# Seven products for eight in half of an MLP's first matrix

## The chip, the cores and the metric

The kernel runs on one core of a Trainium2 chip. The metric is the device time of one execution in microseconds (us). The engines of the core are TensorE (PE in the profile, with its weight loads as PEld), VectorE (DVE), ScalarE (ACT), GpSimd (POOL) and SyncE (SP), each with an instruction queue of its own; SP, ACT and POOL issue DMAs.

## The reference

A trunk of two residual layers over 256 tokens of width 2048, batch 1, in float32. Layer 0 mixes tokens with differential attention, layer 1 with a Mamba-2 mixer; each is followed by an MLP of width 8192. What bears on the change is the MLP:

```python
def sq_relu_mlp(h, w1, w2):
    return jnp.square(jax.nn.relu(h @ w1)) @ w2

for i in range(DEPTH):                       # DEPTH = 2
    hn = rms_norm(h, mixer_norm[i])
    mix = diff_attention(hn, ...) if i % 2 == 0 else mamba2_mixer(hn, ...)
    h = h + mix
    h = h + sq_relu_mlp(rms_norm(h, mlp_norm[i]), mlp_w1[i], mlp_w2[i])
```

`w1` is 2048 x 8192, `w2` is 8192 x 2048.

## The kernel before, in words

All weights come from HBM once, in units of 128 partitions x 1024 float32 (512 KB). `load` (L169) issues the DMA of a unit on SP into a `raw` tile, of which there are six. `split_weights` (L147) makes two float32r parts of it: ScalarE writes the rounded part `wh` (L152), VectorE the remainder `wl = raw - wh` (L153); four buffers each. Activations are split in the same way into a rounded part and a remainder, side by side in an `act` tile. A product is then three matmul terms: rounded by rounded, and the two mixed ones.

There are two forms of a product:

- `sub_block` (L156), for projections whose result has features on partitions: the weights are the stationary side, the activations (both parts side by side, 512 columns) the moving one. Eight matmuls over 512 columns with `wh`, then eight over 256 columns with `wl`. `wide_pair` (L180) runs it four times for two output blocks of 128 features, `wide_one` (L189) twice for one. `add_sums` (L196) then adds the two halves of the bank.
- `token_block` (L202), for projections whose result has tokens on partitions: the activations are stationary, 512 columns of weights move. Per unit and block of 128 tokens: two rounded, two remainder and two mixed matmuls, 12 in all for 256 tokens.

`mlp` (L475) goes through the hidden width in four quarters of 2048. In a quarter the *up stage* makes eight pairs of hidden blocks with `wide_pair`, applies the squared ReLU (L485), and splits the result (`split_pair`, L227) into `hid`. The *down stage* runs `token_block` four times, once for every 512 output columns, over the eight units of `w2` that belong to the quarter, and adds into the residual `h` (L490), with the scale of the norm.

Small work (norm inputs, attention, the scan) is written as generators in a `Side` queue and is emitted by `side.tick()` between matmuls. `norm_input` (L250) transposes a part of `h` on PE and makes `xs`, the split inputs of the next projection, from it (`x_parts`, L235). The code is written against a tile framework: it gives out buffers and semaphores, and when the program is built it also orders each engine's instructions by its own model of time, with the order in the program as priority. On the chip every queue runs in that fixed order.

PSUM is held by two pools for the whole kernel: four banks for `pp`, three for `aux` and one for `aux1`.

Of the kernel before, what the change touches and what calls it, by code (L numbers as in the profile page):

```python
# [82 lines left out]
def wait(n):  # L83
    for _ in range(n):
        yield


@with_exitstack
def trunk_kernel(ctx: ExitStack, tc: tile.TileContext, x, xt, par, rope, qk, wv, wo, w10, w20, win, wdt, wout, w11, w21, out):
# [20 lines left out]
    G.affine_select(out=tri, in_=ones, pattern=[[1, P]], compare_op=ALU.is_ge, fill=0.0, base=0, channel_multiplier=-1)  # L110

    def aux():
        return ps_ax.tile([P, 512], F32, tag="aux", bufs=3, name="aux")

    def aux1():
        return ps_ax.tile([P, 512], F32, tag="aux1", bufs=1, name="aux1")

    def rows(dst, cols, name):

# [23 lines left out]
    def cols(j):  # L143
        return slice(NB * j, NB * (j + 1))


    def split_weights(raw, n=1):  # L147
        wh = wp.tile([P, 1024], F32R, tag="wh", bufs=4, name="wh")
        wl = wp.tile([P, 1024], F32R, tag="wl", bufs=4, name="wl")
        for i in range(n):  # L150
            s = slice(1024 // n * i, 1024 // n * (i + 1))
            S.copy(out=wh[:, s], in_=raw[:, s])  # L152
            V.tensor_tensor(out=wl[:, s], in0=raw[:, s], in1=wh[:, s].bitcast(F32), op=ALU.subtract)  # L153
        return wh, wl
# [13 lines left out]

    def load(src, n=1):  # L169

        raw = wp.tile([P, 1024], F32, tag="raw", bufs=6, name="raw")
        w = 1024 // n
        for i in range(n):
            nc.sync.dma_start(out=raw[:, i * w:(i + 1) * w], in_=src[:, i * w:(i + 1) * w])
        return raw

    def bank():
        return ps.tile([P, 2, T], F32, tag="mm", name="pp")
# [17 lines left out]
    def add_sums(dst, pp):  # L196

        for t in range(len(pp)):
            S.copy(out=dst[:, t, :], in_=pp[t][:, 1, :])  # L199
            V.tensor_tensor(out=dst[:, t, :], in0=pp[t][:, 0, :], in1=dst[:, t, :], op=ALU.add)  # L200

    def token_block(src, j, acts):  # L202

        pp = [bank().rearrange("p a b -> p (a b)") for _ in range(2)]
        n = src.shape[0]
        for s in range(n):
            w = split_weights(load(src[s, j]))
            for i, wi in enumerate(w):
                for k in range(2):
                    while len(acts) <= 2 * s + k:  # L210
                        side.tick()
                    act = acts[2 * s + k]
                    m = wi[:, k * NB:(k + 1) * NB]
                    for t in range(2):
                        tok = slice(t * P, (t + 1) * P)
                        PE.matmul(pp[t], lhsT=act[:, 0, tok], rhs=m, start=(s + i + k == 0), stop=(s == n - 1 and i + k == 2))  # L216
                        if i == 0:
                            PE.matmul(pp[t], lhsT=act[:, 1, tok], rhs=m, start=False, stop=False)  # L218
                    if i == 0 or k:
                        side.tick()  # L220
        return pp

    def act_pair():
        t = actp.tile([P, 2, 2, T], F32R, tag="act", bufs=16, name="act")
# [2 lines left out]
    def split_pair(src):  # L227

        t, parts = act_pair()
        S.copy(out=t[:, :, 0, :], in_=src)  # L230
        V.tensor_tensor(out=t[:, :, 1, :], in0=src, in1=t[:, :, 0, :].bitcast(F32), op=ALU.subtract)  # L231
        return parts
# [44 lines left out]
    def norm_mean():  # L277

        V.tensor_reduce(out=ms, in_=ssq, axis=AX.X, op=ALU.add)
        V.tensor_scalar(out=ms, in0=ms, scalar1=1.0 / D, scalar2=EPS, op0=ALU.mult, op1=ALU.add)  # L280

    def residual(pp, j):
        for t in range(2):
            V.tensor_tensor(out=h[:, t, cols(j)], in0=pp[t], in1=h[:, t, cols(j)], op=ALU.add)  # L284

    xs = []
    first = [bank() for _ in range(2)]
    raw = []  # L290
# [21 lines left out]
    with tc.tile_pool(name="att", bufs=1) as ap:  # L312
# [139 lines left out]
        for hd in range(NH):  # L452
            qkn = ap.tile([P, 4, T], F32, tag="qkn", bufs=2, name="qkn")
            pq = qkn[:, 0:2, :]
            add_sums(pq, wide_pair(qk, 4 * hd, xs) if hd else first)
            side.add(qk_norm(pq, qg, pq))
            pk = qkn[:, 2:4, :]
            add_sums(pk, wide_pair(qk, 4 * hd + 2, xs))
            st = []
            side.add(qk_work(pk, qkn, st))  # L460
            if hd % 2 == 0:
                v2 = ap.tile([P, 2, 2, T], F32, tag="v", bufs=2, name="v")
                for t, pv in enumerate(token_block(wv, hd // 2, xs)):
                    S.activation(v2[:, t], pv.rearrange("p (a b) -> p a b", a=2), AF.Identity, scale=rtok[:, t:t + 1])
            side.add(av_work(hd, v2[:, :, hd % 2, :], qkn, st, heads), slow=True)
        for j in range(4):
            residual(token_block(wo[0:4], j, sum((heads[i] for i in range(4)), [])), j)
        side.drain()
        xs = []
        for j in range(4):  # L470
            residual(token_block(wo[4:8], j, sum((heads[i] for i in range(4, 8)), [])), j)
            side.add(norm_input(j, C_MLP0, xs))


    def mlp(xs, w1, w2, pool, after):  # L475
        r2 = const.tile([P, 2], F32, tag="r2", bufs=2, name="r2")
        for q in range(4):
            hid = []
            for j in range(8):
                r = pool.tile([P, 2, T], F32, tag="relu", bufs=2, name="relu")  # L480
                add_sums(r, wide_pair(w1, 16 * q + 2 * j, xs))
                if q == 0 and j == 1:
                    norm_mean()
                    V.reciprocal(out=r2, in_=ms)
                V.scalar_tensor_tensor(out=r, in0=r, scalar=0.0, in1=r, op0=ALU.max, op1=ALU.mult)  # L485
                hid += split_pair(r)
# [12 lines left out]
            side.add(norm_input(j, C_MIX1, xs_next))  # L499

    with tc.tile_pool(name="mlp0", bufs=1) as mp:
        mlp(xs, w10, w20, mp, to_mixer)
    xs = xs_next


    with tc.tile_pool(name="ssm", bufs=1) as sp:
        dram_a = tc.dram_tile([64, T], F32, name="dram_a")
        rstd = sp.tile([P, T], F32, name="rstd")
# [220 lines left out]
        def out_part(q, last):  # L729
            acts = ys[2 * q] + ys[2 * q + 1]  # L730
            for j in range(4):
                residual(token_block(wout[4 * q:4 * q + 4], j, acts), j)
                if last:
                    side.add(norm_input(j, C_MLP1, xs_next))

# [10 lines left out]
        out_part(3, True)  # L746
    xs = xs_next

    with tc.tile_pool(name="mlp1", bufs=1) as mp:
        mlp(xs, w11, w21, mp, lambda j, t: nc.sync.dma_start(out=out[:, t, cols(j)], in_=h[:, t, cols(j)]))  # L750

def _units(b):

    return np.ascontiguousarray(b.reshape(b.shape[0], P, -1, 1024).transpose(0, 2, 1, 3))


def _blocks(w, order=None):

    k, n = w.shape[0] // P, w.shape[1] // P
    b = w.reshape(k, P, n, P).transpose(2, 1, 0, 3)
    if order is not None:
        b = b[order]
    return _units(b)


def _tokens(w):
# [69 lines left out]
```

## Time and profile before

| | us |
|---|---|
| Median of 3 runs (2512.38 to 2512.57) | 2512.4 |
| The profiled execution | 2510.96 |
| Span of it, first to last instruction | 2509.2 |
| PE busy | 2493.1 (99%) |
| DVE busy | 1668.7 (67%) |
| ACT busy | 1310.0 (52%) |
| POOL busy | 1.2 |
| Moved by DMA | 471.26 MB, mean 188 GB/s |

A group row of the profile reads: line, engine, operation, output <- inputs, shape, xcount | busy us, mean ns of one | idle time of the engine before them, and what ended it. In a timeline row the first number is the start in us, the second how long it took. In the chain of waits a row is a piece of the chain that ended last: its start and the time it gave to the chain. In a table of windows each engine has its busy time and, in brackets, its instructions; the last columns are the granted PE clock, the busy share of the 16 DMA engines, and GB/s.

### The profile page before, as it was taken

The numbers are of one execution on the slowest core, as the hardware profiler recorded it, in microseconds if no ns is written. First come the engines' busy times: TensorE is split into PE (matmuls) and PEld (weight loads), VectorE is DVE, ScalarE is ACT, GpSimd is POOL, SyncE is SP. The second block draws the span as 40 slices with busy tenths as digits, with TensorE's granted clock in tenths as the row PEclk, the third lists the DMA queues.
The fourth block names the chain that finished last, engine by engine and source line by source line (L and its number), as shares of the span: only waits on it lengthen the run. The fifth ranks groups of instructions, "written<-read, shape, count | busy, mean of one in ns | idle before, by whom it ended". The sixth has DMA issues, their size and how long they took to land.

```text
span 2509.2 us, 33804 instructions
## 1 busy us (share of the span) xinstructions
PE 2493.1 (99%) x13038; PEld 2122.0 (85%) x13038; DVE 1668.7 (67%) x2158; ACT 1310.0 (52%) x1919; POOL 1.2 (0%) x8
## 2 busy tenths in 40 slices
PE   8999999999999999999999999999999999999999
PEld 6888888888888888888888888888888888888887
DVE  7888876655555556558886887887665565555554
ACT  6656655434434434456776575674544443443443
POOL 0000000000000000000000000000000000000000
PEclk9999999999999999999999999999999999999999
DMA  8445555555555565556655556455555555656564
GB/s 276 163 157 181 167 176 183 187 193 193 187 193 191 187 199 187 190 179 207 196 186 195 175 188 207 159 186 187 184 190 193 192 186 193 193 188 193 189 197 139
DMA packets 131122, 471.26 MB, mean 188 GB/s; under 512 B 14640, under 2 KB 14832, under 8 KB 130960
## 3 DMA queue, kind: packets, MB, share of 16 engines
q1 hardware_dynamic: 127152, 458.28, 56.1%
q10 hardware_dynamic: 3808, 10.81, 1.3%
q8 instruction: 102, 1.67, 0.3%
q14 instruction: 60, 0.49, 0.1%
HBM read 466.88 MB, written 2.16 MB: 187 GB/s over the span
## 4 chain that ended last, share of the span: by engine, by line
PE 99%; DMA 1%; SPq 0%; issue 0%; DVE 0%; ACT 0%; DVEq 0%
PE pp L162 35%; PE pp L216 28%; PE pp L166 18%; PE pp L218 14%; PE aux L650 1%; PE aux L135 0%; PE aux L397 0%; PE aux L259 0%; DMA raw<-in_qk 0%; PE aux L620 0%; PE aux L651 0%; PE aux L426 0%; DMA xf<-in_x 0%; PE aux L427 0%; PE aux L607 0%; PE aux L420 0%
## 5 line engine op out<-in xcount | busy, mean ns | idle before, releaser
L153 DVE TENSOR_TENSOR wl<-raw,wh 128x1024 fp32r<-128x1024 f32 (+1 forms) x867 | 1057.2, 1222 | 711.0 <-ACT wh L152 704.8
L152 ACT CAST wh<-raw 128x1024 fp32r<-128x1024 f32 (+1 forms) x867 | 908.1, 1049 | 1074.1 <-PE pp L218 507.0
L162 PE MATMUL pp<-act,wh 128*128 128x512 f32 x3856 | 979.3, 394 | 11.8 <-DVE act L241 11.8
L162 PEld LDWEIGHTS pp<-act,wh 128*128 128x128 f32 x3856 | 693.0, 189 | 138.1 <-ACT wh L152 11.1
L216 PE MATMUL pp<-wh,act 128*128 128x512 f32 x1536 | 601.3, 391 | 0.0
L218 PE MATMUL pp<-wh,act 128*128 128x512 f32 x1536 | 599.0, 390 | 0.0
L166 PEld LDWEIGHTS pp<-act,wl 128*128 128x128 f32 x3856 | 524.6, 191 | 37.7 <-issue 1.7
L166 PE MATMUL pp<-act,wl 128*128 128x256 f32 x3856 | 540.8, 283 | 0.0
L216 PE MATMUL pp<-wl,act 128*128 128x512 f32 x1536 | 413.4, 391 | 0.0
L216 PEld LDWEIGHTS pp<-wh,act 128*128 128x128 f32 x1536 | 288.5, 188 | 60.2 <-issue 1.0
L218 PEld LDWEIGHTS pp<-wh,act 128*128 128x128 f32 x1536 | 288.8, 188 | 58.1
L216 PEld LDWEIGHTS pp<-wl,act 128*128 128x128 f32 x1536 | 286.6, 188 | 59.9 <-issue 1.0
L575 DVE SCALAR_TENSOR_TENSOR cy<-u,cwb,cy 128x256 f32<-128x256 f32 x144 | 62.5, 480 | 21.3 <-ACT cy L573 21.2
L490 DVE SCALAR_TENSOR_TENSOR h<-pp,r,h 128x512 f32<-128x512 f32 x64 | 45.1, 747 | 43.0 <-PE pp L216 43.0
L200 DVE TENSOR_TENSOR relu<-pp,relu 128x256 f32<-128x256 f32 x128 | 53.5, 418 | 0.0
L199 ACT COPY relu<-pp 128x256 f32<-128x256 f32 x128 | 46.9, 367 | 0.0
L485 DVE SCALAR_TENSOR_TENSOR relu<-relu 128x512 f32<-128x512 f32 x64 | 44.3, 692 | 2.2
L635 ACT ACTIVATE m<-ab,acol 128x128 f32<-128x128 f32 x128 | 41.6, 391 | 6.7 <-PE aux L651 6.7
L284 DVE TENSOR_TENSOR h<-pp,h 128x512 f32<-128x512 f32 x48 | 31.0, 685 | 19.7 <-PE pp L216 19.7
L231 DVE TENSOR_TENSOR act<-relu,act 128x512 fp32r<-128x512 f32 x64 | 43.9, 686 | 0.0
L230 ACT CAST act<-relu 128x512 fp32r<-128x512 f32 x64 | 39.2, 613 | 0.0
L240 ACT ACTIVATE act<-aux,pa 128x256 fp32r<-128x256 f32 x48 | 21.6, 472 | 12.4 <-DVE act L241 9.4
(175 smaller groups left out, 954.0 us busy)
## 6 DMA issues: line engine op xcount, KB each, us to landing
raw<-in_w SPq DMA_DIRECT2D x512, 512.0 KB, 4.0
raw<-in_win SPq DMA_DIRECT2D x160, 512.0 KB, 3.5
raw<-in_wout SPq DMA_DIRECT2D x64, 512.0 KB, 3.5
raw<-in_qk SPq DMA_DIRECT2D x63, 512.0 KB, 4.2
raw<-in_wv SPq DMA_DIRECT2D x32, 512.0 KB, 3.3
raw<-in_wo SPq DMA_DIRECT2D x32, 512.0 KB, 3.5
ab<-dram_a ACTq DMA_DIRECT2D x16, 512.0 KB, 5.1
xf<-in_x SPq DMA_DIRECT2D x8, 256.0 KB, 6.6
```

What stands on the lines that cost most here:

```text
L152: S.copy(out=wh[:, s], in_=raw[:, s])
L153: V.tensor_tensor(out=wl[:, s], in0=raw[:, s], in1=wh[:, s].bitcast(F32), op=ALU.subtract)
L162: PE.matmul(acc, lhsT=wh[:, k * P:(k + 1) * P], rhs=acts[k0 + k], start=(start and k == 0), stop=False)
L166: PE.matmul(acc[:, 0, :], lhsT=wl[:, k * P:(k + 1) * P], rhs=acts[k0 + k][:, 0, :], start=False, stop=(stop and k == 7))
L199: S.copy(out=dst[:, t, :], in_=pp[t][:, 1, :])
L200: V.tensor_tensor(out=dst[:, t, :], in0=pp[t][:, 0, :], in1=dst[:, t, :], op=ALU.add)
L216: PE.matmul(pp[t], lhsT=act[:, 0, tok], rhs=m, start=(s + i + k == 0), stop=(s == n - 1 and i + k == 2))
L218: PE.matmul(pp[t], lhsT=act[:, 1, tok], rhs=m, start=False, stop=False)
L231: V.tensor_tensor(out=t[:, :, 1, :], in0=src, in1=t[:, :, 0, :].bitcast(F32), op=ALU.subtract)
L485: V.scalar_tensor_tensor(out=r, in0=r, scalar=0.0, in1=r, op0=ALU.max, op1=ALU.mult)
L490: V.scalar_tensor_tensor(out=h[:, t, cols(j)], in0=pp[t], scalar=r2[:, t:t + 1], in1=h[:, t, cols(j)], op0=ALU.mult, op1=ALU.add)
L575: V.scalar_tensor_tensor(out=y[:, i, :], in0=u[:, i, k:k + T], scalar=cwb[:, w + k:w + k + 1], in1=y[:, i, :], op0=ALU.mult, op1=ALU.add)
```

## The change

Half of the hidden columns of a quarter (1024 of 2048, in both MLPs) are made by Strassen's method in its form with few additions (Winograd's): a 2 x 2 block product in seven block products. The blocks are 128 tokens x 128 inputs on the activations' side and 128 inputs x 512 columns on the weights' side; the seven results gather in seven PSUM banks over the eight pairs of input blocks (`seven`), and `seven_out` joins them to 256 tokens x 1024 columns. `sum_parts` makes the four sums on the activations' side once per MLP, as side work. On the weights' side four sums are needed: for two of them the block is first loaded twice by a broadcast DMA, and a DMA issued by GpSimd adds two other blocks to it; VectorE makes the other two. The result has tokens on partitions; `hidden` squares it, transposes it on PE in the down stage, and splits it.

The other half stays with `wide_one`. The two alternate; in the first quarter the seven products start two steps later. In the down stage the units that belong to the second half come first. The host prepares the mixed weight layout (`_mixed`). In the MLPs one PSUM pool with eight banks takes the place of the two pools. Loads have four `raw` buffers in place of six; `wh` and `wl` become one tile `w`, four buffers as before. The unread output `junk` of the norm's squares is bfloat16.

```diff
@@ trunk_kernel
-    ps = ctx.enter_context(tc.tile_pool(name="ps_mm", bufs=4, space=PSUM))
-    ps_ax = ctx.enter_context(tc.tile_pool(name="ps_ax", bufs=3, space=PSUM))
+    psum = {}
+    def psum_pools(stack, one):
+        psum["mm"] = stack.enter_context(tc.tile_pool(name="ps_mm", bufs=8 if one else 4, space=PSUM))
+        psum["ax"] = None if one else stack.enter_context(tc.tile_pool(name="ps_ax", bufs=3, space=PSUM))
...
     def split_weights(raw, n=1):
-        wh = wp.tile([P, 1024], F32R, tag="wh", bufs=4, name="wh")
-        wl = wp.tile([P, 1024], F32R, tag="wl", bufs=4, name="wl")
+        w = wp.tile([P, 2, 1024], F32R, tag="w", bufs=4, name="w")
+        wh, wl = w[:, 0, :], w[:, 1, :]
...
-        raw = wp.tile([P, 1024], F32, tag="raw", bufs=6, name="raw")
+        raw = wp.tile([P, 1024], F32, tag="raw", bufs=4, name="raw")
...
-            junk = const.tile([P, NB], F32, tag="junk", bufs=1, name="junk")
+            junk = const.tile([P, NB], BF16, tag="junk", bufs=1, name="junk")
...
+    def sum_parts(pool, x, dst):
+        a = pool.tile([P, 2, T], F32, tag="relu", bufs=2, name="a")
+        for i in range(2):
+            V.tensor_tensor(out=a[:, i, :], in0=x[i][:, 0, :].bitcast(F32), in1=x[i][:, 1, :].bitcast(F32), op=ALU.add)
+        a11, a21, a12, a22 = (a[:, i, t * P:(t + 1) * P] for i in range(2) for t in range(2))
+        f = pool.tile([P, 4, P], F32, tag="relu", bufs=2, name="asum")
+        yield
+        V.tensor_tensor(out=f[:, 0, :], in0=a21, in1=a22, op=ALU.subtract)
+        V.tensor_tensor(out=f[:, 1, :], in0=f[:, 0, :], in1=a11, op=ALU.subtract)
+        V.tensor_tensor(out=f[:, 2, :], in0=a11, in1=a21, op=ALU.subtract)
+        V.tensor_tensor(out=f[:, 3, :], in0=a12, in1=f[:, 1, :], op=ALU.add)
+        yield
+        sa = pool.tile([P, 2, 4, P], F32R, tag="sa", bufs=8, name="sa")
+        S.copy(out=sa[:, 0], in_=f)
+        V.tensor_tensor(out=sa[:, 1], in0=f, in1=sa[:, 0].bitcast(F32), op=ALU.subtract)
...
+    def seven(pool, src, acts, pp, start, stop):
+        r = pool.tile([P, 7, NB], F32, tag="raw7", bufs=2, name="raw7")
+        nc.sync.dma_start(out=r[:, 3:5, :], in_=src[:, 3:4, :].broadcast_to([P, 2, NB]))
+        nc.sync.dma_start(out=r[:, 0:3, :], in_=src[:, 0:3, :])
+        G.dma_start(out=r[:, 3:5, :], in_=src[:, 0:2, :], accum_op=ALU.add)
+        ws = []
+        def parts(a, n):
+            if n == 2:
+                w = wp.tile([P, 2, 2, NB], F32R, tag="w", bufs=4, name="w")
+            else:
+                w = pool.tile([P, 2, 1, NB], F32R, tag="w1", bufs=2, name="w1")
+            S.copy(out=w[:, 0], in_=r[:, a:a + n, :])
+            V.tensor_tensor(out=w[:, 1], in0=r[:, a:a + n, :], in1=w[:, 0].bitcast(F32), op=ALU.subtract)
+            for i in range(n):
+                ws.append((w[:, 0, i, :], w[:, 1, i, :]))
+        parts(0, 2)
+        parts(2, 2)
+        V.tensor_tensor(out=r[:, 5, :], in0=r[:, 1, :], in1=r[:, 3, :], op=ALU.add)
+        V.tensor_tensor(out=r[:, 6, :], in0=r[:, 5, :], in1=r[:, 2, :], op=ALU.add)
+        parts(4, 2)
+        parts(6, 1)
+        for n, ((ah, al), (wh, wl)) in enumerate(zip(acts, ws)):
+            PE.matmul(pp[n], lhsT=ah, rhs=wh, start=start, stop=False)
+            PE.matmul(pp[n], lhsT=al, rhs=wh, start=False, stop=False)
+            PE.matmul(pp[n], lhsT=ah, rhs=wl, start=False, stop=stop)
+            if n in (1, 3, 5, 6):
+                side.tick()
+
+    def seven_out(pool, pp):
+        p1, p3, p2, p5, p7, p6, p4 = pp
+        u = pool.tile([P, 2, 2, NB], F32, tag="raw7", bufs=2, name="u")
+        a = pool.tile([P, NB], F32, tag="relu", bufs=2, name="ua")
+        b = pool.tile([P, NB], F32, tag="relu", bufs=2, name="ub")
+        S.copy(out=a, in_=p1)
+        V.tensor_tensor(out=u[:, 0, 0], in0=p2, in1=a, op=ALU.add)
+        V.tensor_tensor(out=a, in0=p6, in1=a, op=ALU.add)
+        V.tensor_tensor(out=b, in0=p7, in1=a, op=ALU.add)
+        V.tensor_tensor(out=u[:, 0, 1], in0=p5, in1=a, op=ALU.subtract)
+        V.tensor_tensor(out=u[:, 0, 1], in0=p3, in1=u[:, 0, 1], op=ALU.add)
+        V.tensor_tensor(out=u[:, 1, 1], in0=p5, in1=b, op=ALU.subtract)
+        V.tensor_tensor(out=u[:, 1, 0], in0=p4, in1=b, op=ALU.add)
+        return u
...
+        def hidden(u, hid):
+            V.scalar_tensor_tensor(out=u, in0=u, scalar=0.0, in1=u, op0=ALU.max, op1=ALU.mult)
+            yield from wait(2)
+            uf = u.rearrange("p t a b -> p t (a b)")
+            for j in range(4):
+                ax = aux().rearrange("p (a b) -> p a b", a=2)
+                for f in range(2):
+                    for t in range(2):
+                        PE.transpose(ax[:, f, t * P:(t + 1) * P], uf[:, t, T * j + P * f:T * j + P * f + P], ident)
+                hid += split_pair(ax)
+                yield
+
+        side.add(sums_of(), slow=True)
         for q in range(4):
             hid = []
-            for j in range(8):
-                r = pool.tile([P, 2, T], F32, tag="relu", bufs=2, name="relu")
-                add_sums(r, wide_pair(w1, 16 * q + 2 * j, xs))
...
+            wait_for = 2 if q == 0 else 0
+            for j in range(8 + wait_for):
+                if j >= wait_for:
+                    i = j - wait_for
+                    while len(sas) <= i:
+                        side.tick()
+                    if i == 0:
+                        p7 = [bank().rearrange("p a b -> p (a b)") for _ in range(7)]
+                    seven(pool, w1s[q, i], sas[i], p7, i == 0, i == 7)
+                    if i == 7:
+                        u = seven_out(pool, p7)
+                if j < 8:
+                    if j % 2 == 0:
+                        r = pool.tile([P, 2, T], F32, tag="relu2", bufs=1, name="relu")
+                    add_sums(r[:, j % 2:j % 2 + 1], [wide_one(w1, 8 * q + j, xs)])
+                    if j % 2:
...
+                        V.scalar_tensor_tensor(out=r, in0=r, scalar=0.0, in1=r, op0=ALU.max, op1=ALU.mult)
+                        hid += split_pair(r)
+            side.add(hidden(u, hid))
             for j in range(4):
-                pp = token_block(w2[8 * q:8 * q + 8], j, hid)
+                src = rng(w2, 8 * q + 4, 8 * q + 8) + rng(w2, 8 * q, 8 * q + 4)
+                pp = token_block(src, j, hid)
```

More of the change, by code (lines that the diff above doesn't have):

```diff
@@ L112, in aux @@
     def aux():
-        return ps_ax.tile([P, 512], F32, tag="aux", bufs=3, name="aux")
+        if psum["ax"] is None:
+            return psum["mm"].tile([P, 512], F32, tag="mm", name="aux")
+        return psum["ax"].tile([P, 512], F32, tag="aux", bufs=3, name="aux")
     def aux1():
-        return ps_ax.tile([P, 512], F32, tag="aux1", bufs=1, name="aux1")
+        return psum["ax"].tile([P, 512], F32, tag="aux1", bufs=1, name="aux1")
     def rows(dst, cols, name):
@@ L177, in bank @@
     def bank():
-        return ps.tile([P, 2, T], F32, tag="mm", name="pp")
+        return psum["mm"].tile([P, 2, T], F32, tag="mm", name="pp")
     def wide_pair(src, b, acts):
@@ L204, in token_block @@
         pp = [bank().rearrange("p a b -> p (a b)") for _ in range(2)]
-        n = src.shape[0]
+        n = len(src)
         for s in range(n):
-            w = split_weights(load(src[s, j]))
+            w = split_weights(load(src[s][j]))
             for i, wi in enumerate(w):
@@ L221, in token_block, with rng @@
         return pp
+    def rng(src, a, b):
+        return [src[i] for i in range(a, b)]
     def act_pair():
@@ L466, in trunk_kernel @@
         for j in range(4):
-            residual(token_block(wo[0:4], j, sum((heads[i] for i in range(4)), [])), j)
+            residual(token_block(rng(wo, 0, 4), j, sum((heads[i] for i in range(4)), [])), j)
         side.drain()
@@ L470, in trunk_kernel @@
         for j in range(4):
-            residual(token_block(wo[4:8], j, sum((heads[i] for i in range(4, 8)), [])), j)
+            residual(token_block(rng(wo, 4, 8), j, sum((heads[i] for i in range(4, 8)), [])), j)
             side.add(norm_input(j, C_MLP0, xs))
-    def mlp(xs, w1, w2, pool, after):
-        r2 = const.tile([P, 2], F32, tag="r2", bufs=2, name="r2")
+    scope.close()
+    def sum_parts(pool, x, dst):
[13 more added lines that the diff above has]
+        V.tensor_tensor(out=sa[:, 1], in0=f, in1=sa[:, 0].bitcast(F32), op=ALU.subtract)
+        x0, x1 = x
+        s1, s2, s3, s4 = ([sa[:, i, n, :] for i in range(2)] for n in range(4))
+        dst.append([[x0[:, i, 0:P] for i in range(2)], s4, [x1[:, i, 0:P] for i in range(2)], s1, s3, s2, [x1[:, i, P:T] for i in range(2)]])
+        yield
@@ new lines, in mlp, with sums_of @@
+    def mlp(xs, w1, w1s, w2, pool, after):
+        r2 = const.tile([P, 2], F32, tag="r2", bufs=2, name="r2")
+        sas = []
+        def sums_of():
+            for j in range(KT // 2):
+                while len(xs) < 2 * j + 2:
+                    yield
+                yield from sum_parts(pool, xs[2 * j:2 * j + 2], sas)
+        def hidden(u, hid):
[8 more added lines that the diff above has]
+                hid += split_pair(ax)
+                yield
+        side.add(sums_of(), slow=True)
@@ L477, in mlp @@
         for q in range(4):
             hid = []
-            for j in range(8):
-                r = pool.tile([P, 2, T], F32, tag="relu", bufs=2, name="relu")
-                add_sums(r, wide_pair(w1, 16 * q + 2 * j, xs))
[L482 to L486, printed above, removed]
+            p7 = None
@@ new lines, in mlp @@
+            wait_for = 2 if q == 0 else 0
[14 more added lines that the diff above has]
+                    if j % 2:
+                        if q == 0 and j == 1:
+                            norm_mean()
+                            V.reciprocal(out=r2, in_=ms)
+                        V.scalar_tensor_tensor(out=r, in0=r, scalar=0.0, in1=r, op0=ALU.max, op1=ALU.mult)
+                        hid += split_pair(r)
@@ L501, in trunk_kernel @@
     with tc.tile_pool(name="mlp0", bufs=1) as mp:
-        mlp(xs, w10, w20, mp, to_mixer)
+        with ExitStack() as scope:
+            psum_pools(scope, True)
+            mlp(xs, w10, w10s, w20, mp, to_mixer)
     xs = xs_next
+    scope = ExitStack()
+    psum_pools(scope, False)
     with tc.tile_pool(name="ssm", bufs=1) as sp:
@@ L731, in out_part @@
             for j in range(4):
-                residual(token_block(wout[4 * q:4 * q + 4], j, acts), j)
+                residual(token_block(rng(wout, 4 * q, 4 * q + 4), j, acts), j)
                 if last:
@@ L747, in trunk_kernel @@
     xs = xs_next
+    scope.close()
     with tc.tile_pool(name="mlp1", bufs=1) as mp:
-        mlp(xs, w11, w21, mp, lambda j, t: nc.sync.dma_start(out=out[:, t, cols(j)], in_=h[:, t, cols(j)]))
+        with ExitStack() as scope:
+            psum_pools(scope, True)
+            mlp(xs, w11, w11s, w21, mp, lambda j, t: nc.sync.dma_start(out=out[:, t, cols(j)], in_=h[:, t, cols(j)]))
 def _units(b):
@@ L765, in _blocks, with _mixed @@
     return _units(b)
+def _mixed(w):
+    b = w.reshape(2048, 4, 2, 1024)
+    blocks = _blocks(np.ascontiguousarray(b[:, :, 1]).reshape(2048, 4096))
+    c = b[:, :, 0].reshape(8, 2, P, 4, 2, 512).transpose(3, 0, 2, 1, 4, 5)
+    s = np.stack([c[:, :, :, 0, 0], c[:, :, :, 1, 1], c[:, :, :, 1, 0], c[:, :, :, 0, 1]], axis=3)
+    return blocks, np.ascontiguousarray(s)
 def _tokens(w):
```

12 lines of the change are left out of this document (8 added, 4 removed).

## The prediction

> **What bounds the kernel now.** I read the page's busy table, DMA queues and chain of waits first, to see whether one engine carries the whole span.
>
> ```profile
> span 2509.2 us, 33804 instructions
> ...
> PE 2493.1 (99%) x13038; PEld 2122.0 (85%) x13038; DVE 1668.7 (67%) x2158; ACT 1310.0 (52%) x1919; POOL 1.2 (0%) x8
> ...
> q1 hardware_dynamic: 127152, 458.28, 56.1%
> ...
> PE 99%; DMA 1%; SPq 0%; issue 0%; DVE 0%; ACT 0%; DVEq 0%
> ```
>
> TensorE (PE) is the chain: 99% of it. A busy PE alone proves little, since the ends of matmuls are modelled; that the chain has hardly an entry of another engine is the stronger sign. Then the windows, over the start, the 22 us ahead of the first MLP, and one up stage and one down stage (quarter 1 of the first MLP).
>
> ```profile
> core 0: us, PE busy (x) PEld busy (x) DVE busy (x) ACT busy (x) POOL busy (x), PEclk, DMA share, GB/s
> 0.00:62.00 62.00, 50.18 (x240) 41.12 (x241) 44.61 (x73) 41.06 (x74) 1.24 (x8) 1.00 0.81 277
> 390.00:412.00 22.00, 22.00 (x107) 18.30 (x106) 14.94 (x22) 12.97 (x23) 0.00 (x0) 1.00 0.55 181
> 586.85:676.22 89.37, 89.37 (x514) 78.72 (x513) 54.44 (x63) 41.28 (x55) 0.00 (x0) 1.00 0.59 189
> 676.22:763.28 87.06, 87.06 (x385) 72.12 (x385) 44.98 (x42) 34.52 (x35) 0.00 (x0) 1.00 0.59 193
> ```
>
> An up stage has 32 sub-blocks (8 matmuls over 512 columns, 8 over 256): 89.37/32 = 2.793 us each. PE never idles, at full granted clock; VectorE (DVE) is busy 54.4 of 89.4 us, ScalarE (ACT) 41.3, the DMA engines 0.59. So work taken from PE shortens the stage, until one of these three is full. Last, the pitch of a 512-column matmul whose stationary side changes each time, from the chain in order of time at the end of the last down stage:
>
> ```profile
> 2490.37 1.13 PE pp L216 x5
> ...
> 2493.09 1.13 PE pp L216 x5
> ```
>
> Between the rows lie 12 matmuls (one weight unit): 2.72/12 = 0.2267 us each.
>
> **The PE term.** A quarter has 2048 x 2048 weights. The second half of its columns stays in sub-blocks (`wide_one`, 16 of 2.793 us). The first half was another 16 sub-blocks, 44.7 us; it becomes 8 calls of `seven`, 21 matmuls each, all 512 columns wide and each with its own stationary tile, as in the down stage: 168 x 0.2267 = 38.1 us. Its result has tokens on partitions and has to be transposed, 16 transposes a quarter. Their price, from the timeline where the norm's transposes stand in the matmul stream:
>
> ```profile
> 1075.18 0.60 PE L259 MATMUL aux<-ident,h 128*128 128x128 f32 x4
> 1075.54 0.70 PE L216 MATMUL pp<-wl,act 128*128 128x512 f32 x2
> ```
>
> Four delay the next matmul by 0.36 us: 0.09 each, 1.4 us. PE gains 44.7 - 38.1 - 1.4 = 5.2 us a quarter, 41.4 us in eight. This is the ceiling of the gain; everything below takes from it.
>
> **DVE and ACT in the up stages.** Durations from the groups of that up stage by form, the 128-element price from another group:
>
> ```profile
> L153 DVE TENSOR_TENSOR wl<-raw,wh 128x1024 fp32r<-128x1024 f32 x32 | 39.2, 1225 | 33.7 <-ACT wh L152 33.7
> ...
> L152 ACT CAST wh<-raw 128x1024 fp32r<-128x1024 f32 x33 | 34.6, 1049 | 49.8 <-PE pp L162 28.9 <-issue 19.2 <-PE pp L218 1.7
> L200 DVE TENSOR_TENSOR relu<-pp,relu 128x256 f32<-128x256 f32 x15 | 6.3, 418 | 0.0
> L199 ACT COPY relu<-pp 128x256 f32<-128x256 f32 x15 | 5.5, 367 | 0.0
> L485 DVE SCALAR_TENSOR_TENSOR relu<-relu 128x512 f32<-128x512 f32 x7 | 4.8, 692 | 0.2
> L231 DVE TENSOR_TENSOR act<-relu,act 128x512 fp32r<-128x512 f32 x7 | 4.8, 685 | 0.0
> L230 ACT CAST act<-relu 128x512 fp32r<-128x512 f32 x7 | 4.3, 612 | 0.0
> ```
> ```profile
> L123 DVE TENSOR_SCALAR dge<-ident,em x2: 285/288/291, 32.3 to 32.5; 128x128 f32<-128x128 f32 x2
> ```
>
> One step of the new loop is a `seven` (21 x 0.2267 = 4.76 us of PE) and a `wide_one` (5.59): 10.35 us. DVE per step: the wide half 2 x 1.225 + 0.418 + half of (0.692 + 0.685) = 3.56; `seven` three 1024-splits, one 512-split and the two sums left on the engine, 3 x 1.225 + 3 x 0.685 = 5.73. Together 9.29 of 10.35 us. ACT: 5 x 1.049 + 0.612 + 0.367 + half of 0.612 = 6.5, no bound. The durations overlap a little, by the DVE timeline:
>
> ```profile
> 640.11 1.22 DVE L153 TENSOR_TENSOR wl<-raw,wh 128x1024 fp32r<-128x1024 f32 x1 [1.57 <-ACT wh L152]
> 641.25 0.42 DVE L200 TENSOR_TENSOR relu<-pp,relu 128x256 f32<-128x256 f32 x1
> ```
>
> The next operation starts 1.14 us after a split of 1.22, 0.08 earlier. With that taken off each, a step needs 8.45 us. So DVE goes from 61% to 82-90% of the stage, and PE keeps the lead in quarters 1 to 3. But both queues run in order: a split stuck behind a wait for PE can now reach PE. Cover: 4 split buffers, at least 4.77 us of PE work apart. Between nothing and 1.5 us an up stage I take 0.5, near nothing as the cover exceeds cast plus subtraction (2.3 us): 8 x 0.5 = 4 us.
>
> **Quarter 0** also makes the seven input sums (`sum_parts`): per pair of input blocks 2 x 0.418 + 4 x 0.285 + 0.685 = 2.66 us of DVE, 21.3 in all. Need 8 x 9.29 + 21.3 = 95.6 us by durations, 84.4 by pitches, against 82.8 us of PE: an excess of 1.6 to 12.8 us an MLP. DVE was idle 7 of the 22 us ahead of the stage, when three quarters of the inputs are there, so I take 4, near the lower end: 8 us for both.
>
> **Into the MLP.** `wide_one` asks for the last input blocks one sub-block earlier than the pair of banks did. Rows at the first MLP, DVE except the transposes:
>
> ```profile
> 409.36 1.29 DVE L284 TENSOR_TENSOR h<-pp,h 128x512 f32<-128x512 f32 x2 [1.09 <-PE pp L216]
> ...
> 413.98 0.87 DVE L241 SCALAR_TENSOR_TENSOR act<-aux,pa,act 128x256 fp32r<-128x256 f32 x2
> 415.01 0.88 DVE L241 SCALAR_TENSOR_TENSOR act<-aux,pa,act 128x256 fp32r<-128x256 f32 x2 [0.15 <-ACT act L240]
> ```
> ```profile
> 409.38 1.98 PE L162 MATMUL pp<-act,wh 128*128 128x512 f32 x8
> 411.20 0.60 PE L259 MATMUL aux<-ident,h 128*128 128x128 f32 x4
> ```
>
> Blocks 12 and 13 were ready at 414.9, 14 and 15 at 415.9. The new order wants block 12 at 409.4 + 2.8 + 0.4 + 4 x 0.23 = 413.5 and block 14 at 413.9: 1.4 to 2 us late. I take 1.5, twice 3 us (0 to 4).
>
> **From up to down.** `seven_out` is 7 DVE operations of 512 (4.8 us), two of them possible before the last product; then the squared ReLU over 2048 elements (0.692 + 3 x 0.54 = 2.3 by the step of 512 elements from 0.685 to 1.225), transposes, and cast plus subtraction (1.3): some 8 us, 10 with splits in between. The first four down units, 10.9 us, use the other half's activations and cover it, with 5.6 more in quarters 1 to 3, where a `wide_one` follows. Were the cover gone it would cost 8 x 10 us. In quarter 0 I take 1.5, twice 3 us (0 to 6). The seven banks are freed one by one ahead of need.
>
> **Pools, buffers.** The PSUM pools change at the MLPs' borders; a new bank can wait at most for the pair of residual sums, 1.29 us. Four borders, 0.5 each, near nothing as PE has work queued: 2 us (0 to 5). Loads keep 4 buffers for 6:
>
> ```profile
> L174 SPq DMA_DIRECT2D raw<-in_w x512: 327/328/1387, 384.7 to 2479.1; - x171
> ...
> DMA to landing us min/median/max: 3.1/3.7/8.0
> ```
>
> 4 x 2.72 = 10.9 us against 8.0 for the slowest landing and 2.3 for the split: nothing, but without that cover 1 to 2 us each. `wh` and `wl` in one tile free `wh` 0.95 us later, hidden by the same cover. The bfloat16 `junk` is not read: nothing.
>
> **DMA.** SP issues 4 loads a step as before, 0.33 us each. Two of them fill `raw7`, which has two buffers; behind a load that waits for one stand the `wide_one` loads, with up to 4 raw buffers full. POOL, otherwise empty, waits for the broadcast and issues the accumulate; only the next accumulate is behind it. A `raw7` buffer is free when `seven` i starts, and its accumulated part is wanted some 19 us later; two landings in a row take 7.4 us, 16 at the slowest: hidden. The bytes matter more. At full share the queue row gives 458.28 MB/(0.561 x 2509.2) = 326 GB/s. A slice is 0.262 MB; a step moves 4 for `wide_one`, 5 plain for `seven`, 2 accumulated at an unknown x times the plain price: (9 + 2x) x 0.805 us. x = 1 gives 8.9 us, x = 2 gives 10.5 of 10.35. The trace has no accumulate; nearest is a plain load (x = 1, it cannot be less, as it also reads its target), the far end is one that also takes turns for reading and adding, x = 3. I take the nearest row, x = 1: it costs 0, and so does every x up to 1.9.
>
> The Trainium skill (Collectives: The Full Stack, "The bandwidth ceiling: the fold count and why AG ≠ RS ≠ AR") says that a DMA which adds pushes two source reads through the same ring and so runs at half the rate of a copy. By that rule x = 2, the DMA engines would be just full, and the sum would rise by 64 x 0.12 = 8 us. No run so far shows it.
>
> **Sum.** Profiled execution 2510.96 us (span 2509.2 and 1.8 around it), minus 41.4, plus 4 + 8 + 3 + 3 + 2 = 20: 2489.6. The median of the runs is 1.4 above the profiled one: 2491 us.
>
> **Rivals.**
> - *Everything is hidden* (17%): DVE makes the sums early and no wait reaches PE. For it: 99% now, in stages with DVE at 61%. Against: the late input blocks. 2512.4 - 41.4 = 2471.
> - *DVE is the bound of quarter 0* (15%): 12.8 us by durations, twice, instead of 8: 2491 + 17.6 = 2509. Against it: the overlap of 0.08 us.
> - *The accumulating DMA is slow* (20%, slower): place, the DMA engines in the up stages. It decides from (9 + 2x) x 0.805 = 11.17 - 0.18 (the step before less the transposes), x = 2.3. At x = 3 a step takes 12.1 us: 64 x (12.1 + 0.18 - 11.17) = +70, 2582. For it: 0.59 of the engines is taken already, and 13 slices for 8 come in less time. Against: 277 GB/s at the start at 0.81.
> - *The products gain PE nothing* (3%), were their pitch 0.258 and not 0.2267. Against: loads of 0.19 us fit in the pitch of the down stage. 2512.
>
> The forecast itself, 2481 to 2502, has 45%. Within 0.2% (2507.4 to 2517.4), about the least that can be told from no change, lie half of the second rival and the last. Faster 70% (45, 17 and half of 15), same 10%, slower 20%. Range 2469 to 2521: it holds all but the far part of the DMA case.
>
> **What would show it.** PE 12462 matmuls (13038 - 8 x (256 - 168 - 16)); the up stages 82.8 us for 89.4 but for quarter 0, which is longer; DVE 82-95% in them; PE idle behind `wl` or `sa` if DVE bounds, behind `raw7` or the accumulate if DMA does; DMA share 0.85 to 1.0 there. Wrong if the idle time of PE exceeds 41 us in all, or if the accumulate takes over 10 us to land.

## The result, and the profile after

The changed kernel takes 2728.2 us (median of 4 runs, 2722.13 to 2732.74) against 2512.4 before: a ratio of 1.0858, 95% interval 1.0837 to 1.0879. The prediction, 2491, has the wrong sign, and the time lies outside its range. The page of the changed kernel, in the order in which the page of before was read:

```profile
span 2726.4 us, 33223 instructions
...
PE 2535.0 (93%) x12462; PEld 2111.3 (77%) x12462; DVE 1889.5 (69%) x2494; ACT 1396.3 (51%) x2007; POOL 55.9 (2%) x72
...
q1 hardware_dynamic: 135344, 475.06, 51.2%
q0 software_dynamic: 9216, 33.56, 6.8%
...
PE 65%; DMA 22%; DVE 9%; issue 2%; ACT 1%; SPq 0%; ACTq 0%; POOLq 0%; DVEq 0%; POOL 0%
```

PE has the 12462 matmuls that were expected. But it is idle for 191 us, and where it was 99% of the chain of waits it is now 65%, with 22% DMA and 9% DVE in its place. No engine is full. A window of 90 us in quarter 1 of the first MLP, beside the row of before (89.37 of 89.37 us of PE, DMA share 0.59), shows it in one place:

```profile
626.00:716.00 90.00, 72.97 (x328) 59.46 (x327) 51.43 (x61) 36.27 (x45) 5.11 (x6) 0.89 0.62 182
```

PE is busy 73 of 90 us, DVE 51, the DMA engines 0.62 of the time. Everything has room, so it is a loop of waits. The view of the waits (who waited, for whom, us in total, times, longest):

```profile
ACT w L523 <- DVE raw L532: 376.3, 56, 9.4
...
DVE raw L531 <- DMA raw<-in_w11s: 195.1, 29, 8.8
DVE raw L531 <- DMA raw<-in_w10s: 182.4, 28, 8.3
...
PE pp L538 <- DVE w L524: 150.3, 49, 5.7
```

L531 and L532 are VectorE's two weight sums in `seven`, L523 and L524 the cast and the subtraction of its splits, L536 to L538 its matmuls, L513 and L514 its loads on SP, L515 the accumulating DMA. PE waits 49 times for a split of a `seven`; 57 times VectorE stands at the first weight sum for a DMA, 6.6 us on the mean; ScalarE in turn stands 56 times at a cast that reads the second sum. The chain of waits in order of time says in which order:

```profile
632.98 0.70 DVE raw L531
...
633.71 0.69 DVE raw L532
634.40 1.15 DVE w L524
...
635.56 5.36 DMA raw<-in_w10s
...
641.53 6.21 DMA raw<-in_w10s
...
647.76 0.70 DVE raw L531
...
648.49 0.69 DVE raw L532
649.18 1.15 DVE w L524
...
650.77 5.73 DMA raw<-in_w10s
...
656.64 6.22 DMA raw<-in_w10s
```

From sum to sum lie 14.78 us: two sums (1.4), one split (1.15), the broadcast load (5.4), the accumulate (6.2) and small gaps. The next turn takes 15.1. PE's work for a step is 10.35. VectorE's timeline shows the same turn:

```profile
632.98 0.69 DVE L531 TENSOR_TENSOR raw<-raw 128x512 f32<-128x512 f32 x1 [6.43 <-DMA raw<-in_w10s]
633.71 0.69 DVE L532 TENSOR_TENSOR raw<-raw 128x512 f32<-128x512 f32 x1
634.32 1.82 DVE L524 TENSOR_TENSOR w<-raw,w 128x1024 fp32r<-128x1024 f32 x2
636.06 0.41 DVE L206 TENSOR_TENSOR relu<-pp,relu 128x256 f32<-128x256 f32 x1
636.39 2.35 DVE L159 TENSOR_TENSOR w<-raw,w 128x1024 fp32r<-128x1024 f32 x2
638.66 2.35 DVE L524 TENSOR_TENSOR w<-raw,w 128x1024 fp32r<-128x1024 f32 x2
647.76 0.69 DVE L531 TENSOR_TENSOR raw<-raw 128x512 f32<-128x512 f32 x1 [6.75 <-DMA raw<-in_w10s]
```

What a trace row can't say is to which `raw7` tile an instruction belongs. The order of the built program has the buffer numbers. For two tiles in a row, A and B, VectorE's queue reads:

```
program order in seven()        queue of the changed kernel
A: split 0,1                    A: split 0,1
A: split 2,3                    A: split 2,3
A: sum 5, sum 6                 B: sum 5, sum 6      <- of the next tile
A: split 4,5                    A: split 4,5         <- A's last reader
A: split 6                      B: split 6
B: split 0,1 ...                (wide_one's work)  B: split 0,1 ...
```

(A's own sums and its split 6 stand one turn further up, as B's do here.) The framework ordered the sums of tile B, which need nothing from PE, ahead of the third split of tile A. On ScalarE's queue the cast for B's split 6 likewise stands ahead of `wide_one`'s casts. On the chip these queues are fixed. So A's buffer comes free only when B's accumulate has landed and B's sums are made. Only then may the broadcast into A's buffer go, and the accumulate behind it. The two `raw7` buffers act as one, and the latency of both transfers is paid in full in every turn.

The size agrees. 49 waiting steps x (15.1 - 10.35) = 233 us; the kernel with this order put right by one dependency (e1 below) is 2728.2 - 2483.6 = 245 us faster. In PE's own rows the difference of the two spans, 241 us, is 164 us of more idle time and 77 us of longer busy time for the same 12462 matmuls (2535.0 for 2457.6); the second part goes with a lower granted clock (last section).

### The profile page after: what moved, and what is told of

It is laid out like the page before. It is cut to its first block, busy times and chain, and to the rows that moved or that the text cites. A ratio compares the mean times of both kernels' runs of the same rounds, so it can differ in the third digit from the quotient of the medians.

```text
span 2726.4 us, 33223 instructions
## 1 busy us (share of the span) xinstructions
PE 2535.0 (93%) x12462; PEld 2111.3 (77%) x12462; DVE 1889.5 (69%) x2494; ACT 1396.3 (51%) x2007; POOL 55.9 (2%) x72
## 3 DMA queue, kind: packets, MB, share of 16 engines
q1 hardware_dynamic: 135344, 475.06, 51.2%
q0 software_dynamic: 9216, 33.56, 6.8%
## 4 chain that ended last, share of the span: by engine, by line
PE 65%; DMA 22%; DVE 9%; issue 2%; ACT 1%; SPq 0%; ACTq 0%; POOLq 0%; DVEq 0%; POOL 0%
PE pp L222 22%; PE pp L168 18%; PE pp L224 11%; DMA raw<-in_w10s 11%; DMA raw<-in_w11s 11%; PE pp L172 9%; DVE w L524 3%; DVE raw L531 1%; DVE w L159 1%; DVE raw L532 1%; PE aux L774 1%; PE pp L538 1%; PE aux L576 1%; PE pp L537 1%; PE pp L536 1%
## 5 line engine op out<-in xcount | busy, mean ns | idle before, releaser
L159 DVE TENSOR_TENSOR w<-raw,w 128x1024 fp32r<-128x1024 f32 (+1 forms) x739 | 893.8, 1219 | 310.4 <-ACT w L158 307.3
L158 ACT CAST w<-raw 128x1024 fp32r<-128x1024 f32 (+1 forms) x739 | 769.6, 1050 | 556.1 <-PE pp L222 363.9
L222 PE MATMUL pp<-w,act 128*128 128x512 f32 x3072 | 965.2, 393 | 3.6 <-DVE w L159 3.6
L168 PE MATMUL pp<-act,w 128*128 128x512 f32 x2832 | 743.6, 403 | 17.6 <-DVE act L250 12.8
L222 PEld LDWEIGHTS pp<-w,act 128*128 128x128 f32 x3072 | 575.7, 188 | 124.4 <-DVE w L159 5.3
L168 PEld LDWEIGHTS pp<-act,w 128*128 128x128 f32 x2832 | 531.1, 196 | 124.3 <-ACT w L158 18.2
L224 PE MATMUL pp<-w,act 128*128 128x512 f32 x1536 | 598.8, 390 | 0.0
L523 ACT CAST w<-raw 128x1024 fp32r<-128x1024 f32 (+1 forms) x256 | 235.9, 941 | 524.8 <-DVE raw L532 376.3
L172 PEld LDWEIGHTS pp<-act,w 128*128 128x128 f32 x2832 | 384.7, 190 | 28.7 <-issue 1.7
L172 PE MATMUL pp<-act,w 128*128 128x256 f32 x2832 | 398.1, 283 | 0.0
L224 PEld LDWEIGHTS pp<-w,act 128*128 128x128 f32 x1536 | 288.9, 188 | 58.0
L531 DVE TENSOR_TENSOR raw<-raw 128x512 f32<-128x512 f32 x64 | 44.3, 692 | 377.5 <-DMA raw<-in_w11s 195.1
L524 DVE TENSOR_TENSOR w<-raw,w 128x1024 fp32r<-128x1024 f32 (+1 forms) x256 | 269.6, 1085 | 32.8 <-ACT w L523 31.1
L538 PE MATMUL pp<-w,sa 128*128 128x512 f32 x256 | 117.0, 457 | 149.8 <-DVE w L524 149.8
L538 PEld LDWEIGHTS pp<-w,sa 128*128 128x128 f32 x256 | 53.1, 207 | 180.3 <-DVE w L524 170.3
L537 PE MATMUL pp<-w,sa 128*128 128x512 f32 x256 | 105.9, 414 | 0.0
L536 PE MATMUL pp<-w,sa 128*128 128x512 f32 x256 | 105.8, 413 | 0.0
L538 PE MATMUL pp<-w,act 128*128 128x512 f32 x192 | 82.0, 427 | 0.5 <-DVE w L524 0.5
L537 PE MATMUL pp<-w,act 128*128 128x512 f32 x192 | 82.1, 428 | 0.0
L536 PE MATMUL pp<-w,act 128*128 128x512 f32 x192 | 82.1, 427 | 0.0
L537 PEld LDWEIGHTS pp<-w,sa 128*128 128x128 f32 x256 | 51.4, 201 | 11.5
```

The costliest lines, as they stand in the source:

```text
L168: PE.matmul(acc, lhsT=wh[:, k * P:(k + 1) * P], rhs=acts[k0 + k], start=(start and k == 0), stop=False)
L172: PE.matmul(acc[:, 0, :], lhsT=wl[:, k * P:(k + 1) * P], rhs=acts[k0 + k][:, 0, :], start=False, stop=(stop and k == 7))
L523: S.copy(out=w[:, 0], in_=r[:, a:a + n, :])
L524: V.tensor_tensor(out=w[:, 1], in0=r[:, a:a + n, :], in1=w[:, 0].bitcast(F32), op=ALU.subtract)
L531: V.tensor_tensor(out=r[:, 5, :], in0=r[:, 1, :], in1=r[:, 3, :], op=ALU.add)
L536: PE.matmul(pp[n], lhsT=ah, rhs=wh, start=start, stop=False)
```

## The experiments

Theories: *order* (above); *rate* (the accumulating DMA moves its bytes too slowly, the slow rival of the prediction); *depth* (two landings are too long for two buffers, in whatever order); *side parts* (the new pools and fewer buffers cost).

**e1: the sums behind the second split of their own tile.** A dependency without a semaphore, which only fixes the order:

```diff
-        parts(2, 2)
+        split = parts(2, 2)            # parts() now returns its subtraction
-        V.tensor_tensor(out=r[:, 5, :], in0=r[:, 1, :], in1=r[:, 3, :], op=ALU.add)
+        first_sum = V.tensor_tensor(out=r[:, 5, :], in0=r[:, 1, :], in1=r[:, 3, :], op=ALU.add)
+        tc.add_manual_dep(first_sum.ins, split.ins.name, <NoSync>)
```

> The changed kernel with one edge of order on VectorE: the two weight sums of a tile are queued behind the second split of the same tile, as the program is written, and no longer in front of the third split of the tile before. Order theory (a tile's buffer is held until the third split, which stands behind sums that wait for the next tile's accumulate, so that two buffers act as one and each step costs a broadcast, an accumulate, two sums and a split, 15.1 us): two steps then have 20.7 us for a chain of some 15, PE no longer waits, the step falls to about 10.4 us and the time to 2475 to 2505 us. Rate theory (the accumulating DMA or the DMA engines limit the step): no gain, above 2700. Depth theory (two landings in a row are too long for two buffers, whatever the order): less than a third of the loss comes back, above 2650.

2483.6 us (4 runs, 2480.83 to 2486.85), ratio to before 0.9886, interval 0.9872 to 0.9901. Only that one dependency was edited; in the program built with it, ScalarE's cast for split 6 moved back together with the sums, and a few entries of the other queues moved too. The page, and one up and one down stage (quarter 1 of the first MLP) from its windows:

```profile
PE 2457.6 (99%) x12462; PEld 2070.5 (83%) x12462; DVE 1902.0 (77%) x2494; ACT 1404.1 (56%) x2007; POOL 55.9 (2%) x72
...
q1 hardware_dynamic: 135344, 475.06, 55.9%
q0 software_dynamic: 9216, 33.56, 7.3%
```
```profile
588.15:670.90 82.75, 82.75 (x425) 70.85 (x424) 72.12 (x85) 49.26 (x58) 5.96 (x7) 1.00 0.82 247
670.90:759.83 88.93, 88.93 (x402) 73.65 (x401) 51.53 (x50) 37.29 (x39) 0.86 (x1) 1.00 0.66 220
```

PE never idles in the stage, as the prediction had it: 82.75 us where it said 82.8. The accumulate is as slow as in the changed kernel (6.4 and 7.0 us at the median for the two layers, 6.8 there), and now it is hidden. Rate and depth fall as causes.

**e2: the sums behind the splits of the tile before, no later.** `first_sum` depends on `parts(4, 2)` and `parts(6, 1)` of the preceding call instead.

> The changed kernel with another edge of order: the sums of a tile are queued behind the third and fourth split of the tile before, but still early, in front of the wide half's splits. Order theory: the buffer is free in time, but VectorE still waits at the sums: two steps must hold 12.6 us of landings, then sums and six splits, about 20 to 21 us, so the step is at the edge, 10.4 to 11.2 us, and the time 2485 to 2540. Rate and depth theory: above 2650.

2541.0 us (one run), just over the upper edge. The buffer no longer waits for the next tile's sums, but these sums still stand ahead of their own tile's splits and of the wide half's evictions, and the accumulate hasn't landed when VectorE comes to them. From its waits:

```profile
DVE raw L533 <- DMA raw<-in_w11s: 74.2, 21, 8.3
DVE raw L533 <- DMA raw<-in_w10s: 66.9, 21, 5.7
```
```profile
PE pp L168 <- DVE relu L206: 33.8, 25, 2.5
```

L533 is the first sum here, L206 the eviction of `wide_one`, which queues behind it. So the harm has two parts: the held buffer (2728 to 2541) and the head of an in-order queue standing at a DMA (2541 to 2484).

**e3: an accumulate of 64 columns for 512.** The order is that of the changed kernel; 448 columns of two sums are left out.

```diff
-        G.dma_start(out=r[:, 3:5, :], in_=src[:, 0:2, :], accum_op=ALU.add)
+        G.dma_start(out=r[:, 3:5, 0:64], in_=src[:, 0:2, 0:64], accum_op=ALU.add)
```

> The changed kernel with its order in the loop as it was, but the accumulate adds only 64 of 512 columns (the rest of the two sums is left out). Order theory: the chain of a step loses what the accumulate's landing loses, 6.2 us to an estimated 2.5 to 3, so the step goes from 15.1 to about 11.5 us and the time to 2520 to 2570. Rate theory: a gain as well, down to PE's pace, 2490. Depth theory: landings of 8 us fit two buffers, 2490.

2609.2 us (one run). All three theories forecast a gain, so the direction decides nothing; the size misses the order theory's 2520 to 2570 and is further still from the 2490 of the other two. The chain has the same turn, with a shorter accumulate:

```profile
631.47 0.70 DVE raw L531
...
634.48 5.66 DMA raw<-in_w10s
...
640.16 4.67 DMA raw<-in_w10s
...
644.86 0.70 DVE raw L531
...
657.64 0.70 DVE raw L531
```

Turns of 13.4 and 12.8 us. I had taken the accumulate's time for bytes. The DMA rows (KB each, median us from issue to landing) of the changed kernel, then of e3:

```profile
raw<-in_w10s POOLq DMA_DIRECT2D x32, 512.0 KB, 6.8
```
```profile
raw<-in_w10s POOLq DMA_DIRECT2D x32, 64.0 KB, 4.2
```

With an eighth of the bytes it still takes 4.2 us. By the queue rows, the packets of one accumulate take 2.9 us of the 16 engines' time in the changed kernel (0.068 x 2726.4/64) and 0.7 us in e3, whose page has 4.20 MB at 1.8% for this queue (0.018 x 2607.5/64). So some 3.9 and 3.5 us of the landing are not the moving of bytes, and a higher rate would not shorten them. 49 turns x 2.0 us saved is 98 of the 119 us that were measured.

**e4: the side parts alone**, put into the kernel before: the pool of eight banks in the MLPs, four `raw` buffers, `wh` and `wl` in one tile, bfloat16 `junk`.

> The kernel before with only the small parts of the change: four load buffers for six, both halves of a split weight in one tile, one PSUM pool of eight banks in the MLPs, a bfloat16 output of the norm's squares. All theories and the prediction: these cost 0 to 5 us, 2512 to 2517. If they cost more, part of the loss lies in them and not in the products.

2516.3 us (10 runs), ratio 1.0016, interval 1.0007 to 1.0026: a real cost, and a small one. Its waits of PE, against a single row in the kernel before (`PE pp L162 <- DVE act L241`, 11.8 us, the start):

```profile
PE pp L168 <- DVE act L247: 12.9, 2, 12.4
PE pp L168 <- DVE h L290: 2.5, 2, 1.2
PE pp L168 <- DVE h L499: 1.4, 1, 1.4
```

The last two rows are three pool borders, where the first matmul of the new pool waits for the last residual sums out of the old one: 3.9 us. The buffers show no wait.

**e5: e1 with one PSUM pool of eight banks for the whole kernel.** `psum_pools(ctx, True)` once, and `aux1` from the same pool.

> The kernel is that of e1_late_sums (the two sums queued behind the second split of their own tile), with one PSUM pool of eight banks for the whole kernel in place of one pool for each stage. Border theory: in e1 PE waits at the pool borders for the residual sums (the rows pp L168 <- DVE h of 3.4 us for two and 1.4 us for one), and nothing else in the steady stages; with one pool these waits go, and the time falls by some 4 to 5 us, to about 2479 us (2475 to 2484). Rival: the small products of the norms now share their banks with the large ones and wait for an eviction, which gives the gain back: 2484 us or more.

2481.5 us, ratio 0.9881 (0.9865 to 0.9898). The border waits are gone from the list (e1 has `h L293` 3.4 and `h L614` 1.4 us; here there is none), and the small products don't get in the way. Against e1 the time falls by 2.1 us, within the spread of e1's runs; e7 has the clearer number. (The kernel before, timed beside e1, e5 with e6, and e7, agrees within 0.4 us: 2512.1, 2511.95, 2511.8.)

**e6: no accumulating DMA.** All four sums on VectorE, behind the first split of their own tile:

```diff
-        nc.sync.dma_start(out=r[:, 3:5, :], in_=src[:, 3:4, :].broadcast_to([P, 2, NB]))
-        G.dma_start(out=r[:, 3:5, :], in_=src[:, 0:2, :], accum_op=ALU.add)
+        nc.sync.dma_start(out=r[:, 6, :], in_=src[:, 3, :])
...
+        V.tensor_tensor(out=r[:, 3, :], in0=r[:, 0, :], in1=r[:, 6, :], op=ALU.add)
+        V.tensor_tensor(out=r[:, 4, :], in0=r[:, 1, :], in1=r[:, 6, :], op=ALU.add)
```

> No accumulating DMA: the two tiles that it added into are loaded plainly, and all four weight sums are made by VectorE, queued behind the first split of their own tile. PE's work is unchanged. VectorE's need of a step of 10.35 us rises by two sums of 0.69 us. By durations it is 9.29 + 1.37 = 10.66 us, 0.31 us over the step: 64 steps x 0.31 = 20 us over e1's 2483.6, about 2503 us. By the distance from start to start of its instructions it is 8.45 + 1.37 = 9.8 us, which still fits: about 2484 us (2480 to 2490). Theory of the order (the cause of the slow time is the place of the sums in VectorE's queue): in either case well under the time before, 2480 to 2510. Rival (taking the adding into the transfer is what makes the method pay at all): above 2512 us.

2482.2 us, ratio 0.9882 (0.9868 to 0.9897): the same as e1. The up stage and a few rows of VectorE's timeline:

```profile
588.00:671.00 83.00, 83.00 (x427) 71.06 (x426) 79.53 (x97) 49.58 (x59) 0.00 (x0) 1.00 0.56 200
```
```profile
653.44 0.68 DVE L529 TENSOR_TENSOR raw<-raw 128x512 f32<-128x512 f32 x1
654.04 0.68 DVE L530 TENSOR_TENSOR raw<-raw 128x512 f32<-128x512 f32 x1
654.64 0.69 DVE L532 TENSOR_TENSOR raw<-raw 128x512 f32<-128x512 f32 x1
```

VectorE is busy 96% of the stage, and PE is still never idle. The sums start 0.60 us apart, though each is recorded as 0.68: the pitch is the price, not the duration. By durations VectorE would need 10.66 us of a step of 10.35 and the kernel would take 2503. By pitch it is 8.45 + 2 x 0.60 = 9.65. So the accumulating DMA buys nothing here once the sums are in order. How large the harm would be without the accumulate but in the framework's own order, or with a third `raw7` buffer, is open: neither was run.

**e7: e5 and e6 together.**

> The kernel joins e5 and e6: one PSUM pool for the whole kernel, no accumulating DMA, all four weight sums on VectorE behind the first split of their own tile. If the two edits are independent of each other, the border waits (4.8 us in e6's trace: pp L168 <- DVE h L293 3.4 us, L615 1.4 us) go as they did in e5, and nothing else changes: 2482.2 - 2 to 4.8 = 2477 to 2480 us. Rival: with four sums VectorE has too little room left to evict the small products in time, now that they share their banks with the large ones: 2482 us or more.

2479.0 us (4 runs, 2478.75 to 2479.58), ratio to before 0.9869, interval 0.9852 to 0.9885: the best of all, 33 us under the kernel before. The border waits are gone here too, and its 3.2 us under e6 lie outside the spread of both (e6: 2481.79 to 2484.14).

## Why the prediction was wrong

**The step that failed** is in the paragraph on DMA: "a `raw7` buffer is free when `seven` i starts, and its accumulated part is wanted some 19 us later; two landings in a row take 7.4 us, 16 at the slowest: hidden." The landings of the turn shown were inside these bounds, though not near the 7.4: 12.2 us from the broadcast to the sum (635.56 to 647.76). The cover wasn't there. I had reckoned it from the order of the source, two tiles deep. The built queue put the next tile's sums ahead of this tile's last split, so a buffer came free one tile later, and the cover was nothing. The price of "a split stuck behind a wait" in the paragraph on DVE and ACT is the same miss from the other side: 0.5 us an up stage, bounded at 1.5; it was 31 (245/8). I looked for waits on PE there, and not for a wait on a DMA at the head of VectorE's queue. That the framework orders the queues itself stands in the description of the kernel; I didn't ask what it would do with an operation that is free of PE.

With that order mended (e1) the rest can be read term by term:

| term | predicted, us | e1 shows |
|---|---|---|
| PE's gain in a quarter | 5.2 | 176.43 - 171.68 = 4.75: the up stage gains 6.62 (6.6 predicted), the down stage, where the 16 transposes are, loses 1.87 (1.4 predicted) |
| waits in the up stages of quarters 1 to 3 | 0.5 each | none in quarter 1, where PE is busy throughout |
| quarter 0, and into the MLP | 8 + 3 | `L540 <- ACT w` 2.4 and `L542 <- DVE w` 1.6: 4.0 |
| from up to down | 3 | no such wait |
| pool borders | 2 | 3.4 + 1.4 = 4.8, at three borders; the prediction counted four |

The quarter of before is 586.85 to 763.28, that of e1 588.15 to 759.83. The gain of PE was a little smaller than forecast and the small terms were together too high, so the sum of 2491 would have been 7 us above e1. The profiled execution of e1 is 2486.85 us; 2510.96 - 8 x 4.75 + 4.0 + 4.8 and 2.4 more at the start (14.2 us of waiting for 11.8) give 2484, so some 3 us of it aren't assigned.

**What would show it.** PE's count was right. So were, in e1, the up stage and VectorE's share, 72.12/82.75 = 87%; the DMA share was 0.82, a little under the 0.85 said. The sign named for a wrong forecast, PE idle for more than 41 us, was there; the other, an accumulate of over 10 us to land, was not there at the median (6.8), though the slowest took 11.4. The view of the waits is where it showed first.

**The rivals.** *The accumulating DMA is slow* has the right sign but not the mechanism: x, the price of an accumulated byte in plain ones, is 1.88 (the queue rows give 33.56 MB/(0.068 x 2726.4) = 181 GB/s at full share for q0, 475.06/(0.512 x 2726.4) = 340 for q1), below its point of 2.3, the DMA share is 0.62 where it should be 1, and e1 hides the same accumulates. The Trainium skill (Collectives: The Full Stack, "The bandwidth ceiling: the fold count and why AG ≠ RS ≠ AR") says of the adding step of a ring collective that it reads two sources and so runs at half the rate of a copy. The queue rows of this accumulate, which is no collective, come near that: 1.88 here and 1.85 in e1; my x = 1 was wrong, and it did no harm. *DVE as the bound of quarter 0* falls with e6: by pitch there was room for two sums more in each step. *Everything is hidden*, 2471, is nearest to what the kernel can do: 2479 in e7.

## What to carry to other kernels

Reckon a buffer's cover from the order in which the queues were built, not from the source: of each last reader of a double-buffered tile ask what stands ahead of it in its engine's queue, and whether that waits for the next fill of the other buffer. If so, two buffers are one, and each turn pays the whole latency; no engine is full, and the chain of waits shows transfer, small operation, transfer in a steady period. The mend is the place of one instruction, and moving work off a busy engine onto a transfer is worth a look only once that engine's pitch, not its durations, says that it is full.

## What the runs showed of the hardware

- An accumulating DMA issued by GpSimd ran at 181 to 185 GB/s at full share, against 340 and 342 for the plain queue. An eighth of the bytes (64 KB for 512, in rows of 256 bytes) still took 4.2 us to land for 6.8, and its issue on GpSimd became longer, by these rows of the changed kernel and of e3:

```profile
641.53 0.86 POOL L515 DMA_DIRECT2D raw<-in_w10s  x1 [14.66 <-DVE w L524]
```
```profile
640.16 1.19 POOL L515 DMA_DIRECT2D raw<-in_w10s  x1 [11.68 <-DMA raw<-in_w10s]
```

- A PE that waits often was also granted less clock: 0.89 on the mean of the window shown, where e1's stage has 1.00. The slow matmuls of `seven` start 0.42 us apart, the others 0.23. The length of the gap ahead of them doesn't decide which it is, by rows of the changed kernel: the slow pitch followed a gap of 4.10 us and one of 1.97 us, and the fast pitch a gap of 3.48 us:

```profile
650.37 0.80 PE L538 MATMUL pp<-w,sa 128*128 128x512 f32 x1 [4.10 <-DVE w L524]
650.97 0.63 PE L536 MATMUL pp<-w,sa 128*128 128x512 f32 x1
651.39 0.63 PE L537 MATMUL pp<-w,sa 128*128 128x512 f32 x1
...
665.49 0.50 PE L538 MATMUL pp<-w,sa 128*128 128x512 f32 x1 [1.97 <-DVE w L524]
...
666.11 0.63 PE L537 MATMUL pp<-w,sa 128*128 128x512 f32 x1
666.53 0.63 PE L538 MATMUL pp<-w,sa 128*128 128x512 f32 x1
...
896.50 0.50 PE L538 MATMUL pp<-w,sa 128*128 128x512 f32 x1 [3.48 <-DVE w L524]
896.84 0.39 PE L536 MATMUL pp<-w,sa 128*128 128x512 f32 x1
897.07 0.40 PE L537 MATMUL pp<-w,sa 128*128 128x512 f32 x1
```

  The Trainium skill (TensorE: Matmul & The Clock Gate, "Part 1: The HAM clock gate (the "warmup" mystery)") says that the gate falls to half the PE clock after an idle window of about 3.4 us. The trace agrees on the size of the fall, near one half (0.23 against 0.42 us). It does not show 3.4 us as a limit for a gap: here 1.97 us was followed by the slow pitch, and 3.48 us was not.

- A new PSUM pool cost the first matmul a wait for the last reader of the old one: 1.2 to 1.7 us a border in e4 and e1. With one pool (e5, e7) these waits are gone.
